# A two-layer hybrid encoder on one core: filler per step, the place of two modulation sums, and the queue place of the value loads

## The chip, the cores and the metric

The kernel runs on one core of a Trainium2 chip. The metric is the device time in microseconds (us). The core's engines have queues of their own and each works its queue strictly in order: PE (matrix products and the transposes made with them), DVE (vector), ACT (scalar functions), POOL (elementwise work and the "low halves" of split operands) and SP, whose queue issues all DMAs of this kernel. They wait for each other by semaphores only.

## The reference

Sequence 1024, width 1024, two layers, everything in float32:

```python
for l in range(2):
    shift, scale, gate = split(silu(c) @ ada_w[l] + ada_b[l], 3)
    h = rms_norm(x, norm_g[l]) * (1 + scale) + shift
    if l == 0:   # differential attention (4 heads, two softmax maps each)
                 # beside a bidirectional RG-LRU; both gated; one output projection
        y = even_mixer(h, ...)
    else:        # 2-D neighbourhood attention, 16 heads, 8 x 16 window; gated
        y = odd_mixer(h, ...)
    x = x + gate * y
return rms_norm(x, final_g)
```

## The kernel before

Every large product is done as three products of split operands: an operand is kept as a high half (rounded for PE) and a low half (the remainder), and hi·hi, hi·lo and lo·hi are added up in one PSUM bank. One **projection product** here means one weight slab (128 output rows, 1024 inputs) times one half of the tokens (512): 8 blocks of the input width times 3, so 24 matrix instructions of 128x512. A slab passes three stations before PE can use it: a DMA of 512 KB into `raw` (two buffers), ACT's copy to `whi` (L185), POOL's subtraction to `wlo` (L186).

The kernel runs in stages: a start, the RG-LRU with most of layer 0's projections, layer 0's attention, the "boundary" (layer 0's output projection, the residual sum and layer 1's norm), neighbourhood attention, and the last output projection with the final norm.

**Attention (layer 0).** It is cut into 32 units, one for each head and block of 128 queries. A unit has two sets of logits (tiles `s`, L659 and L660), bias and minimum on DVE (L927), the exponential on ACT (L931), a combination of both maps on DVE and POOL (L946, L948, L949), transposes (`atr`, L957) with their split on ACT and DVE (L964, L965), and for every second unit the product with the values (`o`). Four times in each unit `step()` calls `feed.pump(PUMP)`: a credit of `PUMP` nanoseconds is added, and projection work of a queue called `feed` is put into the program until the credit is spent. The feed holds 19 half-slab products of four pieces with 1300 credit each: 98,800 in all. The loop makes 33 x 4 = 132 steps. At the end of each unit one turn of a modulation generator follows.

**Boundary.** `out_layer(0, ...)` gives `r0` and `r1`: eight projection products for each half of the tokens, over the slabs of `wo0`. The written program is put in order by a scheduler that takes ready instructions by priority, so the first product of `r0` (called pp24 below, the next pp25 and so on up to pp39, by slab) already stands between the last units of attention. Its inputs are the four attention outputs and four RG-LRU outputs `y`, which come back from DRAM (L1128) once attention's key buffers are free, and are split on ACT and POOL (L225, L226). Beside the products, `mod_part` makes two pieces of layer 1's modulation (the scale): each of eight turns loads 256 KB of `ada` (L322) and DVE adds it, weighted, to `macc` (L334, L336); then come `wait` empty turns; then PE sums `macc` over the partitions (tile `mrow`, L368), ACT copies the row (L348), PE turns it into a column (L353) and DVE adds the bias (L356, L358). `wait` is an entry of `NW`. After each product of `r0` three turns are taken. `tail(0, ...)` uses the scale: it makes layer 1's input for the first half of the tokens, one block after another between the products of `r1`.

**Neighbourhood attention (layer 1).** The value projection of two head pairs is one job, `v1_job`: eight blocks of tokens (t = 0 to 7), each evicted to a tile `vt` of two buffers and written to DRAM (`vd`, L1196). `load_v` reads the values back in another order, four blocks for each pair (tiles `vc`, L1208), and `na_c` multiplies with them (tile `no`, L1330). All writes, loads, slabs and biases go through SP's one queue, and an instruction there that waits for a landing holds everything behind it. A load needs the writes of the token blocks that it reads: the first needs t = 5, the second t = 6, the third t = 7.

What sets the order around the change: the numbers `PUMP` and `NW`, the calls of `some(mod, n)` in the boundary, and priorities of the scheduler (`tc.issue_after(x)` gives what follows a place right behind instruction x).

Of the kernel before, what the change touches and what calls it, by code (L numbers as in the profile page):

```python
# [19 lines left out]
P = 128  # L20
# [6 lines left out]
LR = 13  # L27
SQ = 8
NM = (2, 2, 2)
NW = (3, 3, 3, 3)  # L30
KORDER1 = (6, 0, 1, 2, 3, 4, 5, 7)
PUMP = 800.0
PUMP1 = 4400.0
LATE = 3

# [62 lines left out]
def kernel(ctx, tc, xT, xTp, small, lamp, adaw, tb, w0, gw, wo0, w1, nab, wo1, out):  # L98
    nc = tc.nc
# [14 lines left out]
    vd = dram.tile([S, D], F32, tag="vd", name="vd")  # L114
# [17 lines left out]
    def make_sel(pool):  # L132

        sel = state["sel"] = pool.tile([P, 4, P], F32, tag="sel", name="sel", bufs=1)
        G.memset(sel[:], 1.0)
        G.affine_select(sel[:], sel[:], pattern=[[-32, 4], [0, P]], base=0,
                        channel_multiplier=1, compare_op=ALU.is_equal, fill=0.0)
# [11 lines left out]
    state = {"load": 0, "split": 0, "third": None, "turn": 2, "wide": True, "bank": 0}  # L149
# [41 lines left out]
    def slab(i):  # L191
        while state["split"] <= i:
            split_next()
        return ready[i]

    def ahead(i):
        if state["split"] <= i:
            split_next()
# [38 lines left out]
    def proj(i, hf, evac, korder=range(KC), prep=True, view=lambda x: x, cols=(0, HF)):  # L237
        ks = list(korder)
        wh, wl = slab(i)
        ps = bank(f"pp{i}_{hf}")[:, :cols[1] - cols[0]]  # L240
        for n, k in enumerate(ks):
            hi, lo = (t[:, cols[0]:cols[1]] for t in hact[k, hf])
            mm3(ps, wh[:, k, :], wl[:, k, :], view(hi), view(lo), n == 0, n == KC - 1)
            if n % 2 == 1 and n < KC - 1:
                yield 1300.0
        with tc.high_priority():
            evac(hf, ps)
        if prep:
            ahead(i + 1)
        yield 1300.0  # L250
# [362 lines left out]
    def evac_k(key):  # L613
        def f(hf, ps):
            if hf == 0 or (key, 0) not in ks_:
                ks_[key, 0] = kqp.tile([P, S], F32R, tag="ks0", name="ks0")
                ks_[key, 1] = kqp.tile([P, S], F32R, tag="ks1", name="ks1")
            def dst(t, b):
                x = t[b:b + 64, hf * HF:(hf + 1) * HF]
                return x if key[0] == "a" else by_tile(x)  # L620

            def src(b):
                x = ps[b:b + 64, :]
                return x if key[0] == "a" else x.rearrange("p (b g y) -> p b g y", g=2, b=4)

            k0, k1 = ks_[key, 0], ks_[key, 1]
            A.activation(dst(k0, 0), src(0), AF.Copy)
            A.activation(dst(k1, 64), src(64), AF.Copy)
            V.tensor_tensor(dst(k0, 64), src(0), dst(k0, 0), ALU.subtract)
            V.tensor_tensor(dst(k1, 0), src(64), dst(k1, 64), ALU.subtract)  # L630
        return f

    def evac_q(key):

        def f(hf, ps):
            q0 = kqp.tile([P, HF], F32R, tag="qq0", name="qq0", bufs=3)
            q1 = kqp.tile([P, HF], F32R, tag="qq1", name="qq1", bufs=3)

            l0 = kqp.tile([P, HF], F32R, tag="qlo", name="ql0", bufs=3)
            l1 = kqp.tile([P, HF], F32R, tag="qlo1", name="ql1", bufs=3)  # L640
            G.memset(l0[64:128, :].bitcast(F32), 0.0)
            G.memset(l1[0:64, :].bitcast(F32), 0.0)
            A.activation(q0[0:64, :], ps[0:64, :], AF.Copy, scale=0.125)
            A.activation(q1[64:128, :], ps[64:128, :], AF.Copy, scale=0.125)
            V.scalar_tensor_tensor(l0[0:64, :], ps[0:64, :], 0.125, q0[0:64, :],
                                   ALU.mult, ALU.subtract)
            V.scalar_tensor_tensor(l1[64:128, :], ps[64:128, :], 0.125, q1[64:128, :],
                                   ALU.mult, ALU.subtract)
            nc.sync.dma_start(q0[64:128, :].bitcast(F32), q0[0:64, :].bitcast(F32))
            nc.sync.dma_start(q1[0:64, :].bitcast(F32), q1[64:128, :].bitcast(F32))  # L650
            qs_[key, hf] = (q0, q1, l0, l1)
        return f
# [17 lines left out]
    def mods(n, pool, **kw):  # L670

        for _ in range(n):
            yield from mod_part(*later_mods.popleft(), pool, **kw)

    def some(gen, n):
        for _ in range(n):
            next(gen, None)

    def after_dve(gen, n):

        with tc.issue_after(state["dve"]):
            some(gen, n)
# [176 lines left out]
    with ExitStack() as l0:  # L859
# [144 lines left out]
        def step():  # L1004
            if later and next(later[0], 0) == 0:
                later.popleft()
            feed.pump(PUMP)

        mod = mods(NM[1], ap, bufs=1, wait=NW[1])
        for u in range(33):  # L1010
# [97 lines left out]
    def evac_g1(p, pool, tag="sq", late=False):  # L1108
        def f(hf, ps):
            c = slice(hf * HF, (hf + 1) * HF)  # L1110
            t = pool.tile([P, HF], F32, tag=tag, name="sg1", bufs=3)
            if late:
                silu2(hf, ps, t, t)
                state["gated1"][p, hf] = t
                state["gate1"](p, hf)
            else:
                if hf == 0:
                    mix_tile(p, f"sg1_{p}")
                silu2(hf, ps, t, mixed[p][:, c])
        return f  # L1120
# [10 lines left out]
    with tc.tile_pool(name="bound", bufs=2) as bp:  # L1131
        make_sel(bp)
        run, tail = out_layer(0, ato0, xTp, x1d, bp, [4, 5, 6, 7, 0, 1, 2, 3], by_fours, by_tile,
                              ((0, 0, 0, HF), (KC, 1, 0, HF)))
        r0, r1 = run(0), run(1)
        mod = mods(NM[2], bp, bufs=4, wait=NW[2])
        for c in range(KC):
            some(r0, 1)
            after_dve(mod, 3)
        some(mod, 99)  # L1140

        t0 = tail(0, to_h1)
        for c in range(KC):
            some(r1, 1)
            some(t0, (1, 1, 2, 2, 2, 2, 0, 0)[c])
        t1 = tail(1, to_h1)
        ev = {"k": evac_k(("b", 0)), "q": evac_q(("b", 0)), "g": evac_g1(0, bp)}
        first = lambda key, hf: proj(at1[key, 0], hf, ev[key], prep=False)
        ahead(at1["q", 0])
        some(first("k", 0), 99)  # L1150
        some(t1, 1)
        ahead(at1["g", 0])
        some(first("q", 0), 99)
        some(t1, 1)
        for _ in first("g", 0):
            some(t1, 2)
        k1, q1 = first("k", 1), first("q", 1)
        for _ in range(5):
            some(k1, 1)
            some(q1, 1)  # L1160
        ahead(at1["g", 0] + 1)
        some(first("g", 1), 99)
        ahead(at1["g", 0] + 2)
# [3 lines left out]
    with ExitStack() as l1:  # L1167
# [7 lines left out]
        vd4 = vd[:].rearrange("(g y) e -> g y e", g=4)  # L1175

        def v1_job(p):

            i = at1["v", p]
            ws = [slab(i), slab(i + 1)]  # L1180
            for t in range(8):
                hf, b = divmod(t, 4)
                ps = bank("v1")
                for k in range(KC):
                    hi, lo = (t[:, b * P:(b + 1) * P] for t in hact[k, hf])
                    wh, wl = (w[:].rearrange("p (k a) n -> p k (a n)", a=2)[:, k % 4, :]
                              for w in ws[k // 4])
                    mm3(ps[:, :256], hi, lo, wh, wl, k == 0, k == KC - 1)
                    if k == 3:
                        yield 1300.0  # L1190
                vt = ap.tile([P, 256], F32, tag="vt", name="vt", bufs=2)
                if t % 2:
                    A.activation(vt[:], ps[:, :256], AF.Copy)
                else:
                    V.tensor_copy(vt[:], ps[:, :256])
                nc.sync.dma_start(vd4[2 * hf:2 * hf + 2, 64 * b:64 * b + 64, P * p:P * p + 256],  # L1196
                                  vt[:])
                if t == 1:
                    ahead(i + 2)
                yield 1300.0  # L1200

        def load_v(p, b):
            if (p, b) in vch or p == NA_PAIRS:
                return
            w = BLK_W[b]
            vt = vch[p, b] = vp.tile([P, 4, P], F32, tag="vch", name=f"vc{p}_{b}")
            y = slice(4 * BLK_C0[b], 4 * (BLK_C0[b] + w))
            nc.sync.dma_start(vt[:4 * w], vd4[:, y, P * p:P * p + P].rearrange("g y e -> y g e"))  # L1208

        def load_ahead(p):  # L1210

# [133 lines left out]
        n_units = 8 * NA_PAIRS  # L1345
        mod = mods(2, ap, tag="tmp", bufs=3, acc=(ap, "tmp"), wait=NW[3], early=True)
        es, ets = {0: na_a(0)}, {}
        for u in range(n_units + 1):
# [4 lines left out]
            if u % 8 == 2:  # L1353

                p = u // 8
# [138 lines left out]
```

## Time and profile before

| | us |
|---|---|
| three runs | 1206.6, 1210.18, 1210.3 |
| median | 1210.18 |
| the profiled execution | 1210.03 |
| its span, first to last instruction | 1208.0 |
| PE busy in the span | 1151.2 (95%) |
| DVE busy | 728.8 (60%) |
| ACT busy | 566.6 (47%) |
| POOL busy | 387.0 (32%) |

PE is busy almost all the time. What a change can win is the time in which PE stands idle, and the time after it in which the granted clock of PE is lower. The profile's "idle before" and "waits" name the last event that let an engine go on; "issue" there means that the profile shows no event.

### The profile page before, as it was taken

Reading aid. Unit: us, or ns where it says so; the run is one execution under the profiler, and the core shown is the slowest. Engines: PE = TensorE matmul, PEld = TensorE weight load, DVE = VectorE, ACT = ScalarE, POOL = GpSimd, SP = SyncE. Lnnn points to the kernel's source line nnn. Section 1 sums busy time; section 2 is a strip of 40 time slices with the busy share of each in tenths; the row PEclk is TensorE's granted clock in tenths of the full one; section 3 lists DMA queues with packets and bytes.
Section 4 is the critical chain, followed back from the end, with each engine's and each line's share of the span. In section 5 each row is a group of like instructions: output and inputs, shape, how many; then the busy total and the mean of one; then the engine's idle time right before and its main releaser. Section 6 shows DMA issues by size and latency. Waiting matters only on the chain.

```text
span 1208.0 us, 19169 instructions
## 1 busy us (share of the span) xinstructions
PE 1151.2 (95%) x7232; PEld 980.0 (81%) x7232; DVE 728.8 (60%) x1414; ACT 566.6 (47%) x1031; POOL 387.0 (32%) x354
## 2 busy tenths in 40 slices
PE   4999999999999999779999899999999999999996
PEld 3788778888778887657879788988998898888896
DVE  6757949588889889658873244333444434546354
ACT  4357586466555558423433344334444434445121
POOL 2124421332323344524423332332333333216200
PEclk8999999999999999889999999999999999999998
DMA  9723132322121110276523432343445444214212
GB/s 329 228 73 122 51 94 77 94 82 75 38 86 53 58 46 21 67 231 222 179 74 117 130 93 86 94 141 101 128 132 141 136 128 132 78 52 150 99 71 71
DMA packets 82045, 132.26 MB, mean 109 GB/s; under 512 B 7584, under 2 KB 48672, under 8 KB 81952
## 3 DMA queue, kind: packets, MB, share of 16 engines
q1 hardware_dynamic: 81952, 131.03, 34.8%
q8 instruction: 57, 0.93, 0.3%
q14 instruction: 36, 0.29, 0.1%
HBM read 110.03 MB, written 14.68 MB: 103 GB/s over the span
## 4 chain that ended last, share of the span: by engine, by line
PE 78%; DVE 9%; DMA 4%; issue 4%; ACT 3%; POOL 2%; SPq 0%; DVEq 0%; POOLq 0%; ACTq 0%
PE pp L201 16%; PE pp L202 16%; PE pp L203 15%; PE no L1330 3%; PE etr L1312 3%; PE v L201 2%; PE v L202 2%; PE v L203 2%; PE atr L957 2%; DMA vd<-vt 2%; PE s L659 2%; PE s L660 2%; PE n L659 2%; PE n L660 2%; DVE e L927 1%
## 5 line engine op out<-in xcount | busy, mean ns | idle before, releaser
L202 PE MATMUL pp<-alo,whi 128*128 128x512 f32 (+1 forms) x1040 | 395.0, 380 | 3.6 <-POOL alo L226 3.6
L201 PE MATMUL pp<-ahi,whi 128*128 128x512 f32 (+1 forms) x1040 | 397.2, 382 | 0.2 <-DVE ks L630 0.2
L203 PE MATMUL pp<-ahi,wlo 128*128 128x512 f32 (+1 forms) x1040 | 394.8, 380 | 1.0 <-POOL wlo L186 1.0
L186 POOL TENSOR_TENSOR wlo<-raw,whi 128x1024 fp32r<-128x1024 f32 x80 | 197.5, 2472 | 268.5 <-ACT whi L185 254.5
L202 PEld LDWEIGHTS pp<-alo,whi 128*128 128x128 f32 x1040 | 197.1, 189 | 37.6 <-POOL alo L226 4.3
L203 PEld LDWEIGHTS pp<-ahi,wlo 128*128 128x128 f32 x1040 | 196.7, 189 | 38.1 <-POOL wlo L186 1.8
L201 PEld LDWEIGHTS pp<-ahi,whi 128*128 128x128 f32 x1040 | 196.9, 189 | 35.7 <-issue 2.1
L1301 POOL TENSOR_SCALAR e<-e,r 128x288 f32<-128x288 f32 (+1 forms) x128 | 71.3, 570 | 239.7 <-DVE r L1299 239.3
L185 ACT ACTIVATE whi<-raw 128x1024 fp32r<-128x1024 f32 x80 | 84.3, 1056 | 121.0 <-PE pp L202 65.7
L1296 ACT ACTIVATE e<-e,nm 128x288 f32<-128x288 f32 (+1 forms) x128 | 72.7, 569 | 51.3 <-DVE nm L1293 50.7
L931 ACT ACTIVATE e<-e,nm 128x1024 f32<-128x1024 f32 x64 | 73.5, 1149 | 47.7 <-DVE nm L927 45.5
L1293 DVE CUSTOM_DVE_ANT_0 e<-n,bias 128x288 f32<-128x288 f32 (+1 forms) x128 | 60.4, 504 | 51.9 <-PE n L660 32.2
L1318 DVE COPY e<-etr 96x384 f32<-96x384 f32 (+1 forms) x64 | 35.5, 554 | 91.1 <-PE etr L1312 89.5
L1316 ACT ACTIVATE e<-etr 96x384 f32<-96x384 f32 (+1 forms) x64 | 31.3, 490 | 118.9 <-DVE e L1318 118.5
L927 DVE CUSTOM_DVE_ANT_0 e<-s,tb 128x1024 f32<-128x1024 f32 x64 | 77.1, 1219 | 10.1 <-PE s L660 9.1
L201 PE MATMUL v<-whi,ahi 128*128 128x256 f32 x256 | 72.2, 282 | 0.0
L203 PE MATMUL v<-whi,alo 128*128 128x256 f32 x256 | 71.9, 281 | 0.0
L202 PE MATMUL v<-wlo,ahi 128*128 128x256 f32 x256 | 71.9, 281 | 0.0
L948 POOL TENSOR_SCALAR e<-e,r 128x256 f32<-128x256 f32 x32 | 33.9, 1059 | 110.1 <-DVE r L937 47.2
L964 ACT ACTIVATE ath<-atr 128x512 fp32r<-128x512 f32 x64 | 37.7, 596 | 40.4 <-PE atr L957 40.0
L1062 DVE SCALAR_TENSOR_TENSOR xh<-pp,mod,xh 128x512 f32<-128x512 f32 (+1 forms) x40 | 25.7, 641 | 50.8 <-PE pp L203 49.9
L1067 ACT ACTIVATE sq<-xh 128x512 f32<-128x512 f32 (+1 forms) x40 | 21.7, 543 | 72.8 <-DVE xh L1062 71.9
(207 smaller groups left out, 2076.4 us busy)
## 6 DMA issues: line engine op xcount, KB each, us to landing
raw<-in_w_dram SPq DMA_DIRECT2D x56, 512.0 KB
ada<-in_adaw_dram SPq DMA_DIRECT2D x96, 256.0 KB
raw<-in_wo_dram SPq DMA_DIRECT2D x24, 512.0 KB
bias<-in_nab_dram SPq DMA_DIRECT2D x64, 144.0 KB
qq<-qq SPq DMA_DIRECT2D x48, 128.0 KB
bias<-in_nab_dram SPq DMA_DIRECT2D x32, 192.0 KB
xT<-in_xT_dram SPq DMA_DIRECT2D x16, 256.0 KB
xh<-in_xTp_dram SPq DMA_DIRECT2D x16, 256.0 KB
```

Of the source, the lines that this page charges most:

```text
L185: A.activation(hi[:], raw[:], AF.Copy)
L186: G.tensor_tensor(lo[:], raw[:], hi[:], ALU.subtract)
L201: T.matmul(ps, lh, rh, start=start, stop=False)
L202: T.matmul(ps, lh, rl, start=False, stop=False)
L203: state["pe"] = T.matmul(ps, ll, rh, start=False, stop=stop).ins
L659: T.matmul(dst, qsel(q[m]), k, start=True, stop=False)
L660: T.matmul(dst, qsel(q[2 + m]), k, start=False, stop=True)
L927: state["dve"] = V.tensor_tensor_reduce(out=e[:], in0=ps[:].rearrange("p a b -> p (a b)"), in1=tbt[h][:, o:o + S], scale=-1.0, scalar=3.0e ...
L931: A.activation(e[:], e[:], AF.Exp, scale=-1.0, bias=nm[:], accum_out=sums[:, m:m + 1])
L1293: state["dve"] = V.tensor_tensor_reduce(out=e[:, m, :n], in0=ps[:, m, :n], in1=bias["now"][m][:, :n], scale=-1.0, scalar=3.0e38, op0=ALU.a ...
L1296: A.activation(e[:, m, :n], e[:, m, :n], AF.Exp, scale=-1.0, bias=nm[:, m:m + 1], accum_out=sums[:, m:m + 1])
L1301: state["pool"] = G.tensor_scalar(e[:, m, :n], e[:, m, :n], r[:, m:m + 1], 0.0, ALU.mult, ALU.add).ins
```

## The change

Three independent edits.

1. `PUMP` falls from 800 to 745. Over 132 steps that is a credit of 98,340 instead of 105,600, against 98,800 of work: the attention filler is dealt out more thinly and reaches the loop's end instead of ending in the 31st unit.
2. The third entry of `NW` rises from 3 to 7, so each of the boundary's two modulation pieces takes 16 turns instead of 12. The first piece's sum on PE now follows the sixth product of `r0`, not the fourth. The second piece no longer ends before `r1`: its last waits and its sum are taken behind the first and second product of `r1`.
3. `load_v` stands in `tc.issue_after(state["vd"])`, where `state["vd"]` is the last write of a value block so far.

```diff
-NW = (3, 3, 3, 3)
+NW = (3, 3, 7, 3)
-PUMP = 800.0
+PUMP = 745.0
...
             after_dve(mod, 3)
-        some(mod, 99)
...
             some(r1, 1)
+            some(mod, (4, 99)[c] if c < 2 else 0)
             some(t0, (1, 1, 2, 2, 2, 2, 0, 0)[c])
...
-                nc.sync.dma_start(vd4[2 * hf:2 * hf + 2, 64 * b:64 * b + 64, P * p:P * p + 256],
-                                  vt[:])
+                state["vd"] = nc.sync.dma_start(
+                    vd4[2 * hf:2 * hf + 2, 64 * b:64 * b + 64, P * p:P * p + 256], vt[:]).ins
...
-            nc.sync.dma_start(vt[:4 * w], vd4[:, y, P * p:P * p + P].rearrange("g y e -> y g e"))
+            with tc.issue_after(state["vd"]):
+
+                nc.sync.dma_start(vt[:4 * w],
+                                  vd4[:, y, P * p:P * p + P].rearrange("g y e -> y g e"))
```

On PE, behind the last logits of attention (`s_1_4660`, the second map of the last unit), there stood so far the first output product pp24 (`pp_0_4880`), whose third input block is already the reloaded `y` tile `ahi_0_4820`; `obc` and `atr` belong to attention:

```order
L660 MATMUL s_1_4660<-ks_3055,ql_3474 128x512
L201 MATMUL pp_0_4880<-ahi_0_4812,whi_4471 128x512
L202 MATMUL pp_0_4880<-alo_0_4813,whi_4471 128x512
L203 MATMUL pp_0_4880<-ahi_0_4812,wlo_4472 128x512
L201 MATMUL pp_0_4880<-ahi_0_4816,whi_4471 128x512
L397 MATMUL obc<-osq,sel 128x128 x4
L957 MATMUL atr<-ident,e_0_4490 128x128 x4
L202 MATMUL pp_0_4880<-alo_0_4817,whi_4471 128x512
L203 MATMUL pp_0_4880<-ahi_0_4816,wlo_4472 128x512
L201 MATMUL pp_0_4880<-ahi_0_4820,whi_4471 128x512
```

Now there stands the feed's last half-slab product (`pp_1_4648`, the last gate), whose inputs were made long before:

```order
L660 MATMUL s_1_4632<-ks_3126,ql_3597 128x512
L201 MATMUL pp_1_4648<-ahi_1_489,whi_4328 128x512
L202 MATMUL pp_1_4648<-alo_1_490,whi_4328 128x512
L203 MATMUL pp_1_4648<-ahi_1_489,wlo_4329 128x512
L201 MATMUL pp_1_4648<-ahi_1_494,whi_4328 128x512
L202 MATMUL pp_1_4648<-alo_1_495,whi_4328 128x512
L203 MATMUL pp_1_4648<-ahi_1_494,wlo_4329 128x512
L201 MATMUL pp_1_4648<-ahi_1_634,whi_4328 128x512
L397 MATMUL obc<-osq,sel 128x128 x4
L957 MATMUL atr<-ident,e_0_4446 128x128 x4
```

All 24 instructions of that product now come behind the last logits, and pp24 behind them. So 24 product instructions fewer stand ahead of the last logits. Behind attention's last `obc` there were 3 instructions of pp25 left so far, and there are 21 now.

On SP, in the boundary, the slab of pp29 (`raw_5052`) stood behind the write of the residual block 3 (`x1d<-xh_0_3`):

```order
L1065 DMA x1d<-xh_0_2_4925 128x512
L322 DMA ada<-in_adaw_dram 128x512 x2
L1053 DMA xh_0_4_5016<-in_xTp_dram 128x512
L1065 DMA x1d<-xh_0_3_4972 128x512
L156 DMA raw_5052<-in_wo_dram 128x1024
L1053 DMA xh_0_5_5062<-in_xTp_dram 128x512
L156 DMA raw_5098<-in_wo_dram 128x1024
L322 DMA ada<-in_adaw_dram 128x512 x3
```

Now the slabs of pp29 and pp30 (`raw_5052`, `raw_5090`) are ahead of that write:

```order
L1065 DMA x1d<-xh_0_2_4925 128x512
L322 DMA ada<-in_adaw_dram 128x512 x2
L1053 DMA xh_0_4_5016<-in_xTp_dram 128x512
L156 DMA raw_5052<-in_wo_dram 128x1024
L1053 DMA xh_0_5_5054<-in_xTp_dram 128x512
L156 DMA raw_5090<-in_wo_dram 128x1024
L1065 DMA x1d<-xh_0_3_4972 128x512
```

The write of block 3 and three loads of the second modulation piece moved behind the slabs.

On SP, in the first value job of layer 1, the loads `vc` stood between the last writes (the row `x3` ends with t = 5):

```order
L1196 DMA vd<-vt 2x64x256 x3
L1208 DMA vc_0_6210<-vd 96x4x128
L1196 DMA vd<-vt 2x64x256
L1208 DMA vc_1_6212<-vd 128x4x128
L156 DMA raw_6454<-in_w_dram 128x1024
L1196 DMA vd<-vt 2x64x256
L1269 DMA bias<-in_nab_dram 128x288
L1269 DMA bias<-in_nab_dram 128x384
L156 DMA raw_6584<-in_w_dram 128x1024
L1208 DMA vc_2_6214<-vd 128x4x128
```

Now all writes come first, up to t = 7, with one slab between the last two:

```order
L1196 DMA vd<-vt 2x64x256 x4
L156 DMA raw_6454<-in_w_dram 128x1024
L1196 DMA vd<-vt 2x64x256
L1210 DMA vc_0_6210<-vd 96x4x128
L1210 DMA vc_1_6212<-vd 128x4x128
L1272 DMA bias<-in_nab_dram 128x288
L1210 DMA vc_2_6214<-vd 128x4x128
L1210 DMA vc_3_6216<-vd 96x4x128
L1272 DMA bias<-in_nab_dram 128x384
```

The two loads went behind the writes of t = 6 and t = 7, and the third and fourth went ahead of one bias load and one slab. The other three value jobs change in the same way; in the last of them only one load moves. On PE, DVE, ACT and POOL nothing is moved in layer 1.

## The prediction

> **What bounds the kernel now.** The page comes first: busy times of the engines, then the span in 40 slices of 30.2 us.
>
> ```profile
> span 1208.0 us, 19169 instructions
> PE 1151.2 (95%) x7232; PEld 980.0 (81%) x7232; DVE 728.8 (60%) x1414; ACT 566.6 (47%) x1031; POOL 387.0 (32%) x354
> PE   4999999999999999779999899999999999999996
> PEclk8999999999999999889999999999999999999998
> ```
>
> PE is the bound nearly everywhere. The two 7s in its row, with two 8s in the clock row below, are 483 to 543 us: the end of attention and the start of the boundary. The edits touch nothing else that waits, except the value loads from 640 on. So the second view is windows of 5 us at these places. The columns are the busy us of PE, PEld, DVE, ACT and POOL, then the granted clock, the DMA share and GB/s.
>
> ```profile
> 470.00:475.00 5.00, 4.56 (x36) 2.97 (x34) 4.96 (x9) 4.19 (x8) 1.18 (x2) 1.00 0.00 0
> 475.00:480.00 5.00, 3.31 (x10) 2.83 (x11) 4.45 (x11) 1.77 (x3) 2.06 (x3) 0.67 0.00 0
> 485.00:490.00 5.00, 2.40 (x18) 2.08 (x18) 4.79 (x11) 4.74 (x5) 3.58 (x5) 1.00 0.56 193
> 490.00:495.00 5.00, 1.39 (x7) 0.67 (x5) 5.00 (x8) 2.95 (x5) 5.00 (x5) 0.88 0.00 2
> 495.00:500.00 5.00, 4.96 (x22) 4.87 (x23) 3.04 (x5) 1.18 (x3) 4.19 (x3) 0.50 0.02 3
> 525.00:530.00 5.00, 2.51 (x12) 1.74 (x10) 4.94 (x6) 0.63 (x1) 2.45 (x1) 1.00 0.92 291
> 530.00:535.00 5.00, 0.15 (x4) 0.18 (x8) 4.14 (x7) 0.63 (x1) 0.00 (x0) 0.63 0.94 280
> 535.00:540.00 5.00, 5.00 (x20) 3.67 (x16) 0.16 (x1) 1.33 (x2) 0.46 (x1) 0.50 0.90 302
> 540.00:545.00 5.00, 5.00 (x21) 4.04 (x20) 0.72 (x2) 0.90 (x1) 1.91 (x1) 0.84 0.72 257
> 680.00:685.00 5.00, 4.33 (x40) 3.47 (x38) 0.47 (x2) 0.51 (x2) 0.00 (x0) 1.00 0.56 192
> 685.00:690.00 5.00, 2.27 (x24) 1.81 (x24) 2.03 (x4) 2.62 (x6) 3.33 (x3) 0.83 0.76 205
> 690.00:695.00 5.00, 5.00 (x21) 4.33 (x20) 1.90 (x6) 1.31 (x4) 0.88 (x2) 0.83 0.30 98
> 795.00:800.00 5.00, 4.17 (x54) 3.35 (x54) 1.12 (x4) 1.11 (x3) 0.99 (x2) 1.00 0.76 202
> ```
>
> PE's idle time in a window is 5.00 less its first number; what a low clock costs is that busy number times (1 - clock). **Tail of attention**: idle 0.44 + 1.69 + 2.60 + 3.61 = 8.3, clock 3.31 x 0.33 + 1.39 x 0.12 + 4.96 x 0.50 = 3.7, together 12.0 us. **Boundary**: idle 2.49 + 4.85 = 7.3, clock 5 x 0.50 + 5 x 0.16 = 3.3, together 10.6. **Value loads**: idle 0.67 + 2.73, clock 2.27 x 0.17 + 5 x 0.17 = 1.2, and 0.83 at 795, together 5.5. The sum, 28.1 us, is the ceiling of the whole change: PE's own work stays what it is.
>
> Third, the waits of PE: who released it, total us, times, longest.
>
> ```profile
> PE mrow L368 <- issue: 7.3, 1, 7.3
> PE pp L202 <- POOL alo L226: 3.6, 2, 3.2
> PE obc L397 <- DVE osq L384: 2.6, 1, 2.6
> PE atr L957 <- DVE atl L965: 1.9, 1, 1.9
> PE no L1330 <- DMA vc<-vd: 4.2, 3, 3.4
> ```
>
> Each edit has its wait: the modulation sum (mrow) 7.3, the value loads (vc) 4.2. The tail is mixed: 3.6 us for the reloaded y blocks split on POOL, but 4.5 us for DVE.
>
> **Edit 1, the filler.** No instruction is added. 24 product instructions leave the front of the last logits, so units come to their end earlier if DVE can follow.
>
> ```profile
> 400.00:450.00 50.00, 50.00 (x316) 41.72 (x315) 43.21 (x97) 27.59 (x52) 17.09 (x19) 1.00 0.20 63
> ```
>
> Here PE is full and DVE has 6.8 us of 50 left, so the units before the tail do speed up. In the tail it is the other way round: DVE is busy 4.96, 4.45, 4.79 and 5.00 of 5, so more PE work there does not make DVE's chain shorter. What the last gate product behind the last logits covers for certain is the wait for y: 24 instructions are more than the 3.6 us. With it would go the half clock that follows it at 495:500, 2.5 us. That is one end, 6.1. The other end is 0: the last combine, which waits for DVE, makes PE wait as long at the same place. I take 3.5, a little above the middle, because the y wait is certain to be covered and only the DVE wait behind it is open. For the range the ends are 0 and all 12.0.
>
> **Edit 2, the sums.** Here are the sum's own rows on DVE and PE, and SP, ACT and POOL on the slab of pp29, with the evictions of pp28 and pp29 as last rows.
>
> ```profile
> 514.76 1.16 PE L397 MATMUL obc<-osq,sel 128*128 128x128 f32 x8
> 530.04 0.42 SPq L1053 DMA_DIRECT2D xh<-in_xTp_dram  x1
> 532.62 0.38 SPq L156 DMA_DIRECT2D raw<-in_wo_dram  x1
> 534.00 0.74 DVE L336 SCALAR_TENSOR_TENSOR macc<-ada,ctmp,macc 128x512 f32<-128x512 f32 x1
> 534.85 0.65 PE L368 MATMUL mrow<-macc,ones 128*32 128x128 f32 x8 [7.34 <-issue]
> 538.41 1.06 ACT L185 ACTIVATE whi<-raw 128x1024 fp32r<-128x1024 f32 x1 [2.57 <-DMA raw<-in_wo_dram]
> 539.54 2.37 POOL L186 TENSOR_TENSOR wlo<-raw,whi 128x1024 fp32r<-128x1024 f32 x1 [12.09 <-ACT whi L185]
> 544.28 0.75 DVE L1062 SCALAR_TENSOR_TENSOR xh<-pp,mod,xh 128x512 f32<-128x512 f32 x1 [7.61 <-PE pp L203]
> 549.72 0.75 DVE L1062 SCALAR_TENSOR_TENSOR xh<-pp,mod,xh 128x512 f32<-128x512 f32 x1 [0.23 <-PE pp L203]
> ```
>
> "issue" hides the releaser, but mrow starts 0.1 us after DVE's eighth accumulation has ended (534.74): the sum asks for macc too early. A product takes 549.72 - 544.28 = 5.44 us, so two products later the sum asks 10.9 us later, at 538.4 by the old clock, and macc is there. **What is late next** is the slab of pp29: ACT waits for its DMA until 538.41, and the DMA engines are at 0.92 and 0.94. So far this lies under the 7.34 us. Counted from the obc at 514.76, which is shortly before the boundary's loads may start: the slab is issued at +17.9, split by ACT from +23.7 and by POOL until +27.2 (541.91). In the new order it follows xh directly, so it is issued at 530.46 or +15.7, 2.2 us sooner, with whi done at +22.6 and wlo at +25.0. PE has 1.16 of obc, then 21 + 72 instructions at 5.44 / 24 = 0.227 until pp29: +22.2. It waits 0.4 for whi, makes two products, and waits for wlo until +25.0: 2.4 us idle, though with 18 instructions (4.1 us) of its work moved behind the obc. The new place has a price too. The row of the sum is copied by ACT behind the split of the slab of pp31, itself a DMA; PE's L353 waits behind 4 instructions of pp30, and DVE's L356 behind that. I estimate 1.0 us, the length of one split (1.06). The second sum, L353 behind the first bc, costs under 0.5, and the scale it gives is needed only by layer 1's first product, six products later. So the boundary's 10.6 becomes 2.4 + 1.0 and a half microsecond of clock: gain 6.7, with ends 2 (the slab comes no sooner) and 10.6.
>
> The 535:540 row shows the clock at 0.50 behind 7.34 us of idle, and the 475:480 row 0.67 in and around 1.69. The Trainium skill ("TensorE: Matmul & The Clock Gate", "What's actually happening") says that PE falls to half clock after an idle window of about 3.4 us and needs as long a busy one to recover. The first row agrees, the second does not need that much idle. By the page the 2.4 us cost no clock and the gain is 7.2; by the second row 1.1, and it is 6.1.
>
> **Edit 3, the loads.** SP's queue of the first value job, POOL, and the end of the chain of work:
>
> ```profile
> 669.28 2.42 POOL L186 TENSOR_TENSOR wlo<-raw,whi 128x1024 fp32r<-128x1024 f32 x1 [9.68 <-issue]
> 670.15 0.34 SPq L1208 DMA_DIRECT2D vc<-vd  x1
> 670.53 0.49 SPq L1196 DMA_DIRECT2D vd<-vt  x1
> 675.62 0.39 SPq L1208 DMA_DIRECT2D vc<-vd  x1
> 676.11 0.86 SPq L156 DMA_DIRECT2D raw<-in_w_dram  x1
> 677.06 0.50 SPq L1196 DMA_DIRECT2D vd<-vt  x1
> 677.06 6.54 DMA vd<-vt
> 683.61 4.08 DMA vc<-vd
> ```
>
> The second load sits in the queue until 675.62, where the write of t = 6 has landed, and the slab and the write of t = 7 behind it. Then come 6.54 us of landing and 4.08 of load, until 687.69. Without the loads ahead of it the slab waits only for POOL's split, which ends at 671.70; the write of t = 7 follows at about 672.3, 4.8 us sooner, and the third load lands at 672.3 + 6.54 + 4.08 = 682.9. PE went idle at 684.3 (685 - 0.67), so the wait goes with 1.4 us to spare. The biases and the slab behind the loads are issued 1 to 2 us later than now; what hides them is PE's work, and if that is not enough they cost as much. Of 5.5 I take 4.7; the ends are 0 and 5.5.
>
> **Sum.** 3.5 + 6.7 + 4.7 = 14.9. From the profiled execution's 1210.03 that is 1195.1, so I say **1195**; the median of the runs shown, 1210.18, is the same to 0.2, while one of them was 1206.6.
>
> **Rivals.**
> *The tail goes entirely.* Against it stand DVE's full windows; for it, that the units come earlier and y is loaded earlier. 12.0 + 6.7 + 4.7 = 23.4: 1187.
> *New waits take the place of the old ones.* DVE holds the tail (0), the slabs hold the boundary (2), only the loads are won (4.7): 1203. For it: DVE busy at 5.00 and the DMA share of 0.94 in the very windows that are to be won.
> *The change doesn't do what it says.* The loads land together and late, the sums wait at L353: under 3 us, 1208.
> *Slower.* DVE becomes the bound of all of attention: with less filler each unit waits for DVE once, as at 475:480, where one such wait cost 1.69 + 1.1 = 2.8 us. It decides where the 28 units before the tail lose 14.9 / 28 = 0.53 us each on average; at 0.7 it is 19.6 lost, 1215. Against it: the 6.8 us that DVE has free in 50.
>
> **How the numbers follow.** Forecast 0.52, tail gone 0.20, new waits 0.17, nothing 0.07, slower 0.04. About 0.3%, 3.6 us, can be told from no change, so all below 1206.5 counts as faster: 0.89, same 0.07, slower 0.04. The range runs from 1185, two below the tail's case, to 1206, three above the case of new waits; what is left out is nothing, slower, and the edges.
>
> **What would show it.** In the changed profile: no wait of mrow near 7 us, a PE wait of 2 to 3 us on wlo or whi in pp29; the pp L202 wait on alo gone and PE still idle before the last atr of attention; the wait of no on vc under 1 us, with t = 7 written within 5 us of t = 6. I am wrong if PE's idle time grows before the tail, if the boundary's slabs make it wait more than once, or if the last combine costs nothing.

## The result, and the profile after

The changed kernel took 1196.8 us (median of 7 runs, 1194.3 to 1203.9) beside 1209.3 of the kernel before: ratio 0.9911, 95% interval 0.9888 to 0.9935. A second set of runs gave 1197.9 beside 1207.1: 0.9923 (0.9900 to 0.9947). So by these ratios the change wins 9.3 to 10.7 us of about 1208 (the medians of the two sets lie 12.5 and 9.2 apart); a gain of 14.9 had been forecast. The profiled execution took 1195.79; its start happened to come 2.0 us sooner than that of before, as the ledger below shows.

The page of after: span, busy times, then PE and its clock in 40 slices of 29.9 us.

```profile
span 1194.1 us, 19182 instructions
PE 1145.0 (96%) x7232; PEld 975.6 (82%) x7232; DVE 728.8 (61%) x1414; ACT 566.9 (47%) x1031; POOL 387.7 (32%) x354
PE   4999999999999999799999999999999999999996
PEclk8999999999999999899999999999999999999998
```

Of the two 7s one is left, the end of attention; the boundary's is gone. PE has as many instructions as before. Its busy time is 6.2 us shorter, and the granted clock accounts for 5.6 of that: busy time x (1 - clock), summed over windows of 5 us, is 13.6 us before and 8.0 after.

The windows that answer to those of before (busy us of PE, PEld, DVE, ACT, POOL, then clock, DMA share, GB/s):

```profile
350.00:400.00 50.00, 45.10 (x259) 37.74 (x258) 42.04 (x82) 26.38 (x48) 13.73 (x15) 0.97 0.23 70
475.00:480.00 5.00, 3.50 (x16) 2.57 (x14) 5.00 (x9) 5.00 (x7) 4.64 (x4) 1.00 0.57 172
480.00:485.00 5.00, 1.39 (x6) 1.39 (x7) 5.00 (x6) 0.76 (x1) 3.32 (x4) 0.61 0.09 38
485.00:490.00 5.00, 5.00 (x27) 4.42 (x26) 3.83 (x6) 3.17 (x5) 0.32 (x1) 0.71 0.00 0
490.00:495.00 5.00, 4.04 (x29) 3.38 (x27) 4.51 (x6) 5.00 (x10) 2.80 (x2) 1.00 0.01 2
495.00:500.00 5.00, 3.97 (x23) 3.22 (x24) 4.83 (x9) 4.81 (x8) 3.61 (x4) 1.00 0.01 3
530.00:535.00 5.00, 2.31 (x10) 1.30 (x9) 2.25 (x4) 3.15 (x4) 2.59 (x2) 1.00 0.75 288
535.00:540.00 5.00, 5.00 (x16) 3.94 (x16) 2.64 (x1) 0.00 (x0) 2.09 (x1) 0.66 0.81 252
685.00:690.00 5.00, 5.00 (x28) 4.17 (x26) 1.74 (x5) 2.19 (x6) 1.15 (x2) 1.00 0.45 111
```

The value loads' stretch (685) is full. The boundary has one short stall. The tail still stands idle with DVE at 5.00 of 5. And the first row is new: 4.9 us idle in the middle of attention, 3.1 at a product `s` and 1.8 at the next obc. The same window of before:

```profile
350.00:400.00 50.00, 49.22 (x291) 41.38 (x290) 44.22 (x86) 27.99 (x49) 15.05 (x14) 1.00 0.20 63
```

The waits of PE in after (total us, times, longest) name the largest of these. Of the 7.2 at obc, 5.1 stand in the tail and 1.8 in the middle of attention; of the 2.8 on wlo, 1.7 stand in the boundary's stall, and the other 1.1, near 607 us, had been 1.0 before:

```profile
PE obc L397 <- DVE osq L384: 7.2, 3, 5.1
...
PE s L659 <- DVE nm L927: 3.1, 1, 3.1
PE pp L203 <- POOL wlo L186: 2.8, 2, 1.7
...
PE pp L201 <- ACT whi L185: 1.0, 1, 1.0
```

For a ledger I cut every profile at three marks: the first logits product of attention (L659), the last obc of attention (**T0**) and the first value product of layer 1. Loss is summed over windows of 5 us between the marks: 5 less PE's busy time, plus busy time x (1 - clock). The last 50 us before T0 are the tail. "Start" is the time up to the first mark, which no edit touches. All in us:

| profile | start | attention's body | tail | boundary | rest |
|---|---|---|---|---|---|
| before | 227.3 | 3.3 | 12.5 | 12.5 | 16.3 |
| after | 225.3 | 7.3 | 9.3 | 5.8 | 11.1 |
| after less before | -2.0 | **+4.0** | -3.2 | -6.7 | -5.2 |

PE's own work at full clock is 936.1 us before and 935.3 after, so the columns make up 13.1 of the 13.9 us between the spans. Of the tail's 3.2, idle time is the smaller part: it fell from 8.4 to 7.3, the loss by the clock from 4.1 to 2.1. The start is chance: over the 14 profiles of this study it lies between 224.9 and 228.5, whatever the kernel.

### The profile page after: what moved, and what is told of

Its sections match the earlier page's. It is cut to its first block, busy times and chain, and to the rows that moved or that the text cites. A ratio compares the mean times of both kernels' runs of the same rounds, so it can differ in the third digit from the quotient of the medians.

```text
span 1194.1 us, 19182 instructions
## 1 busy us (share of the span) xinstructions
PE 1145.0 (96%) x7232; PEld 975.6 (82%) x7232; DVE 728.8 (61%) x1414; ACT 566.9 (47%) x1031; POOL 387.7 (32%) x354
## 4 chain that ended last, share of the span: by engine, by line
PE 77%; DVE 12%; ACT 4%; DMA 3%; issue 2%; POOL 1%; SPq 0%; DVEq 0%; ACTq 0%; POOLq 0%
PE pp L201 15%; PE pp L202 15%; PE pp L203 15%; PE no L1333 4%; PE etr L1315 3%; PE v L201 3%; PE v L203 2%; PE v L202 2%; DVE e L927 2%; PE n L659 2%; PE atr L957 2%; PE n L660 2%; PE s L659 1%; PE s L660 1%; POOL wlo L186 1%
## 5 line engine op out<-in xcount | busy, mean ns | idle before, releaser
L927 DVE CUSTOM_DVE_ANT_0 e<-s,tb 128x1024 f32<-128x1024 f32 x64 | 77.5, 1219 | 11.3 <-DMA tb<-in_tb_dram 4.6
L659 PE MATMUL s<-ks,qq 128*128 128x512 f32 x128 | 52.8, 413 | 3.1 <-DVE nm L927 3.1
```

The source lines that it names most:

```text
L659: T.matmul(dst, qsel(q[m]), k, start=True, stop=False)
L927: state["dve"] = V.tensor_tensor_reduce(out=e[:], in0=ps[:].rearrange("p a b -> p (a b)"), in1=tbt[h][:, o:o + S], scale=-1.0, scalar=3.0e ...
```

## Experiments

Each was timed beside the kernel before (its median 1207.1 to 1208.4 in the three sets), and its loss was taken at the same marks:

| run | ratio to before, 95% | body | tail | boundary | rest |
|---|---|---|---|---|---|
| e1, filler alone | 0.9992 (0.9977 to 1.0007) | 7.6 | 9.4 | 9.0 | 15.9 |
| e2, sums alone | 1.0012 (0.9995 to 1.0029) | 3.3 | 12.5 | 13.0 | 16.5 |
| e3, after without loads | 0.9975 (0.9957 to 0.9993) | 8.2 | 9.5 | 5.8 | 15.6 |
| e4, tb in pieces | 0.9903 (0.9887 to 0.9919) | 6.1 | 9.4 | 7.5 | 10.0 |
| e5, splits on DVE | 0.9952 (0.9922 to 0.9981) | 8.8 | 7.7 | 12.3 | 10.0 |
| e6, thin ada | 0.9887 (0.9858 to 0.9916) | 7.6 | 9.4 | 2.4 | 10.5 |
| e7, fewer Newton steps | 0.9904 (0.9871 to 0.9938) | 7.7 | 5.1 | 4.4 | 10.2 |
| e8, obc later | 0.9898 (0.9860 to 0.9936) | 8.0 | 8.7 | 4.4 | 10.0 |
| after, again | 0.9923 (0.9900 to 0.9947) | 8.0 | 9.4 | 6.0 | 10.5 |
| e9, tb and ada | 0.9878 (0.9852 to 0.9904) | 4.1 | 9.4 | 2.4 | 10.2 |
| e10, tb, ada and obc | 0.9873 (0.9843 to 0.9903) | 4.1 | 9.6 | 2.5 | 9.9 |
| e11, old filler, thin ada | 0.9930 (0.9908 to 0.9953) | 3.3 | 12.5 | 11.3 | 9.4 |

The ratio is of several runs, the loss of one profile each. Before lost 44.6 in all four columns. For e3, e7 and e9 the gain by the ledger lies above the upper end of the ratio's interval, by 0.3, 1.6 and 0.6 us; the profiled executions of e7 and e9 were the fastest of their sets. So the ledger says where time went, and the ratio what a kernel is worth.

### The edits one by one

**e1**, the filler alone:

```diff
-PUMP = 800.0
+PUMP = 745.0
```

> The kernel before with the thinner filler alone (745 for 800). Theory A: the start of the boundary, the obc behind attention, comes 5.6 us sooner (509.12 for 514.76 in the trace of after), and the boundary runs by its DMAs from there on, so that the 18 product instructions (4.1 us) that were moved behind the obc lie inside the wait of mrow, which shrinks from 7.3 to about 3.2. Time about 5.6 under the kernel before: ratio 0.995. Theory B, the prediction's terms taken apart as they stand: the edit wins 2.7 in the tail and loses about 5 in attention's body to the wait for tb (0 to 3.5 by the prediction), mrow waits 7 as before. Ratio 0.997 to 1.002.

**e2**, the sums alone:

```diff
-NW = (3, 3, 3, 3)
+NW = (3, 3, 7, 3)
...
-        some(mod, 99)
...
+            some(mod, (4, 99)[c] if c < 2 else 0)
```

> The kernel before with the sums two products later alone. Theory A: PE comes to pp29 18 instructions sooner, at +18 us from the obc, while its slab is split at +25 as in after: PE waits 6 to 7 us for whi and wlo in place of mrow's 7.3, and the clock falls behind it. Gain 1 to 3: ratio 0.9975 to 0.999. Theory B, the prediction's term: the wait is 2 to 3 us, gain 6.2 to 6.7, ratio 0.9945 to 0.995.

In e1, T0 came 284.0 us behind the first mark, 3.4 sooner than before (287.4), mrow waited 4.3 in place of 7.3, and the boundary lost 3.5 less although no edit was made there. In e2 the wait of mrow is gone and this stands in its place: PE's rows at pp29, and two windows of e2.

```profile
539.09 0.80 PE L201 MATMUL pp<-ahi,whi 128*128 128x512 f32 x1 [6.19 <-ACT whi L185]
541.52 0.79 PE L203 MATMUL pp<-ahi,wlo 128*128 128x512 f32 x1 [1.21 <-POOL wlo L186]
```

```profile
535.00:540.00 5.00, 0.91 (x2) 0.50 (x2) 1.19 (x2) 1.69 (x2) 0.88 (x1) 0.73 0.87 297
540.00:545.00 5.00, 3.79 (x9) 2.80 (x9) 0.00 (x0) 1.06 (x1) 3.79 (x2) 0.50 0.55 184
```

On the waits theory A comes out in both: mrow shrinks in e1 (to 4.3, where 3.2 was expected), and in e2 there are 7.4 us of waiting for the slab of pp29 in place of 7.3 for mrow. On the time it misses in both: e1's 0.9992 is in theory B's range, since attention's body lost 4.3 more, and e2's 1.0012 is above both. Neither edit alone can be told from nothing in time (e1 wins 1.0 by its ratio, between -0.8 and 2.8), while the two together (e3) win 3.0 (0.8 to 5.2). In e2 PE stands at the slab from +19.0 us behind T0 and has whi at +25.2; in after it comes at +22.3 and has whi at +23.3. So the slab is split at a time that does not follow PE's pace (it is issued at +18.8 in e2 and at +16.2 in after); the 18 products (4.1 us) that the thinner filler leaves behind T0 are what covers most of it once the sums no longer stand in the way. In the ledger the boundary gains 3.5 by the filler, loses 0.5 by the sums, and gains 6.7 by both.

**e3**, after with the loads as before:

```diff
-            with tc.issue_after(state["vd"]):
-                nc.sync.dma_start(vt[:4 * w], ...)
+            nc.sync.dma_start(vt[:4 * w], ...)
```

> The kernel after, with the value loads issued without their place behind the last value write, as before. If the loads are worth what the two traces differ in from 640 us on, the waits of no on vc come back with 4 us and the time rises by 5.3 (prediction's term 4.7): 1202, ratio to before 0.994 to 0.995. Rival: the other two edits shift the value jobs so that the waits don't come back; ratio 0.991 as after.

The waits on vc came back with 3.1 us, and the rest of the kernel, from the first value product on, took 563.6 us, as in before (563.7), e1 (563.4) and e2 (564.1). In the profiles that have the edit it took 555.7 to 557.7. So the edit is worth 6 us or more by the length of this stage, and 6.3 to 7.7 by the ratios (0.9975 less 0.9911 or 0.9923), more than the 5.3 expected; the ledger finds 4.5 to 5.1 of it as idle time and clock.

### What the filler cost in attention

The load of the third head's bias table (tb, 960 KB) on SP and the first bias and minimum of that head on DVE, before:

```profile
354.61 0.33 SPq L855 DMA_DIRECT2D tb<-in_tb_dram  x1
361.83 1.21 DVE L927 CUSTOM_DVE_ANT_0 e<-s,tb 128x1024 f32<-128x1024 f32 x1
```

The same two in after, and the product on PE that waits for DVE:

```profile
349.49 0.33 SPq L855 DMA_DIRECT2D tb<-in_tb_dram  x1
357.11 1.22 DVE L927 CUSTOM_DVE_ANT_0 e<-s,tb 128x1024 f32<-128x1024 f32 x1 [3.67 <-DMA tb<-in_tb_dram]
358.40 0.80 PE L659 MATMUL s<-ks,qq 128*128 128x512 f32 x1 [3.13 <-DVE nm L927]
```

The table has one buffer, so its load is issued when the last unit of the head ahead has read the old one. Before, the new head needed it 7.2 us behind the issue; in after, with less filler between, it would have 4.0 us behind it (357.11 - 3.67 - 349.49), and got it after 7.6. **e4** loads it in pieces, as the units of the old head leave its columns:

```diff
...
+            if m and h < DA_HEADS - 1:
+                if qt == 6:
+                    tb_cols(h + 1, 1024, 1920)
+                if qt == 7:
+                    tb_cols(h + 1, 896, 1024)
+                    tb_cols(h + 1, 0, 896)
```

> The kernel after, with the bias table of a head (tb) loaded in three pieces, the first one unit sooner and the one that the head's first unit needs besides it, 64 KB, next. Theory A: the wait of DVE for tb (4.6 us, the new idle time of PE at 350 to 400) is what the thinner filler cost in attention's body; without it the obc behind attention comes 4 to 6 us sooner and the time falls by as much: 1191 to 1193, ratio 0.985 to 0.987. Rival: DVE was about to be late there anyway (24.0 of 25 us busy at 375 to 400); PE waits as long for DVE a few units on, and the gain is under 1.5: ratio 0.990 or 0.991.

DVE's wait fell from 3.67 to this, in e4:

```profile
354.22 1.23 DVE L931 CUSTOM_DVE_ANT_0 e<-s,tb 128x1024 f32<-128x1024 f32 x1 [0.93 <-DMA tb<-in_tb_dram]
```

PE's wait fell to 0.4, and T0 stood 282.2 us behind the first mark in place of 283.8. That is less than half of theory A, and the boundary gave back 1.7. The time, 0.9903, is what the rival had said, but its mechanism does not account for it: at the next obc PE waited 2.0 us for DVE, and 1.8 in after too. In e9, with the same attention, DVE had no wait for tb left, the body lost 4.1 and T0 came at 279.8 (280.3 in e10): there theory A's 4 us are whole. The middle of attention in e9, whole and where the next obc stands:

```profile
350.00:400.00 50.00, 47.47 (x294) 39.97 (x296) 46.47 (x91) 29.47 (x55) 14.83 (x16) 1.00 0.23 64
375.00:380.00 5.00, 3.00 (x20) 2.42 (x19) 4.83 (x9) 1.57 (x3) 3.86 (x3) 1.00 0.64 143
```

The 2.0 us at the obc are there too, but the clock stays at 1.00, where e4 had 0.85 and 0.81 in the two windows from 375 to 385. Of the 2.0 us between the two bodies 1.4 are clock and 0.6 idle time; why the clock fell in one and not in the other is open.

That the thin filler and the load in one piece cost 3 to 4 us in attention is shown by the profiles: the body loses 7.3 to 8.8 in the eight with both, 3.3 in the three with the old filler (before, e2, e11), and 4.1, 4.1 and 6.1 in the three with the load in pieces. The timed runs don't show this size: e4 is 1.0 to 2.4 us under after by the ratios and e9 1.1 under e6, with intervals wider than that.

### What holds the tail

**e7** leaves two of three Newton steps out of the inverse root behind the tail's obc, **e8** moves that obc behind other work, **e5** takes POOL's splits of y to DVE:

```diff
-            rr = rstd_rows(ss, 128, ap, sq, 0.0)
+            rr = rstd_rows(ss, 128, ap, sq, 0.0, 1 if h == 3 and hf == 0 else 3)   # e7
...
+            rr_ins = [state["pe"]]                                                 # e8
...
+            if h == 3 and hf == 0:
+                yield
+                yield
+                yield
-            spread(rr, bc)
+            with tc.issue_after(state["pe"] if h == 3 and hf == 0 else rr_ins[0]):
+                spread(rr, bc)
...
-                          G if l == 0 and k >= 4 else V, order)
+                          V, order)                                                # e5
```

> The kernel after, with two of three Newton steps left out in the inverse root that the obc in the tail waits for (six 128x128 operations of DVE; the half of one head is scaled with less precision). They took 4.3 us there, 3.2 of it two rows of 1.60 beside POOL. The order on PE changes with it: the obc is placed one logit product sooner. Theory A: DVE's queue holds the tail; with 4.3 us less in it the tail loses 3 to 4 us less and the last obc comes as much sooner: ratio 0.988 to 0.989. Theory B: the y blocks (their load, POOL's splits) or the combine are late next; the wait moves on to atr or pp, less than 1.5 us is won: 0.990 or 0.991.

> The kernel after, with that obc of the tail placed later on PE, behind both transposes of unit 30, which now stand ahead of the last logits; no work is added or left out. Theory A (DVE's queue holds the tail): PE waits for DVE at the transposes instead, and the idle time of the tail stays within 1.5 us of after's 7.3; time within 1.5 us of after, ratio 0.990 to 0.992. Theory B (the obc stands too early on PE, and there is other work that it keeps back): the wait of 5.1 goes, idle time in the tail falls by 3 or more, ratio 0.988 or less.

> The kernel after, with the low parts of the reloaded y blocks (8 subtractions, 128x512) on DVE instead of POOL. PE's order has the same products, 13 of them ahead of the last obc instead of behind it. Theory A: in the tail DVE is held up beside POOL's subtractions (L383 takes 1.60 beside them and 0.28 alone, L226 2.44 and 0.7 to 1.1), 7 us in all at 470 to 500, more than the 8 x 0.69 = 5.5 us that DVE would take over; the stretched rows are gone, the wait of obc falls from 5.1 to 3 or less, and the tail loses 3 to 5 us less. Since the slab of pp29 comes at +25 from the last obc whatever PE does, the time follows the last obc: 1 to 3 us under after, ratio 0.989 to 0.990. Theory B: DVE's own work is the bound, 5.5 us more of it on DVE makes the wait of obc longer (7 or more) and the time 2 to 5 us longer: ratio 0.993 to 0.995.

DVE's rows in after's tail, with POOL's two splits of y at the same time:

```profile
475.21 2.44 DVE L226 TENSOR_TENSOR alo<-vT,ahi 128x512 fp32r<-128x512 f32 x1
477.58 1.60 DVE L383 TENSOR_TENSOR osq<-osq 128x128 f32<-128x128 f32 x1
480.35 0.28 DVE L383 TENSOR_TENSOR osq<-osq 128x128 f32<-128x128 f32 x1
481.96 1.60 DVE L384 SCALAR_TENSOR_TENSOR osq<-osq 128x128 f32<-128x128 f32 x1
```

```profile
475.07 3.96 POOL L226 TENSOR_TENSOR alo<-y,ahi 128x512 fp32r<-128x512 f32 x2 [4.60 <-ACT ahi L225]
481.65 1.76 POOL L226 TENSOR_TENSOR alo<-y,ahi 128x512 fp32r<-128x512 f32 x1
```

The same operation takes 0.28 alone and 1.60 beside POOL. The Trainium skill ("SBUF — State Buffer", "SBUF: two separate sides") says that a DVE operation with two SBUF inputs and a POOL operation that reads SBUF exclude each other for a whole instruction. The rows agree, and so does e5, where POOL splits no y there:

```profile
479.48 1.09 DVE L226 TENSOR_TENSOR alo<-y,ahi 128x512 fp32r<-128x512 f32 x1
480.49 0.28 DVE L383 TENSOR_TENSOR osq<-osq 128x128 f32<-128x128 f32 x1
...
482.55 0.28 DVE L384 SCALAR_TENSOR_TENSOR osq<-osq 128x128 f32<-128x128 f32 x1
```

The stretched rows are gone, and the wait of 5.1 at the obc with them:

```profile
485.63 1.16 PE L397 MATMUL obc<-osq,sel 128*128 128x128 f32 x8 [1.50 <-DVE osq L384]
```

But DVE has eight more operations in the tail, and PE waits for it elsewhere: 1.4 at the transposes behind this obc, 1.3 at later ones, and 2.1 at the last obc, where another row of DVE's chain is stretched beside a slab split of POOL (509.89 to 512.29; the row took 0.23 in after):

```profile
510.12 2.25 DVE L379 TENSOR_SCALAR osq<-osq 128x128 int32<-128x128 int32 x1
```

The idle time of the tail is 7.7 us, for 7.3 in after. That its loss is 7.7 for 9.3 is the clock, which stayed at 1.00 in e5 and cost 2.1 in after. And 13 products stand ahead of T0 again, so that at pp29 of e5 PE waits longer:

```profile
541.23 0.79 PE L201 MATMUL pp<-ahi,whi 128*128 128x512 f32 x1 [6.46 <-ACT whi L185]
543.67 0.80 PE L203 MATMUL pp<-ahi,wlo 128*128 128x512 f32 x1 [1.22 <-POOL wlo L186]
```

The boundary loses 12.3. Theory A was right on the stretched rows and on the wait at the obc, and wrong on the idle time of the tail and on the time, which came out as theory B had it from another cause. The expectation took the slab's time from T0 as fixed, and it is not: from T0 = 515.4 the slab is issued at +18.4 (+16.2 in after) behind three ada loads that held SP's queue for 5.0 us, and PE has whi at +25.8. To the missing cover of 3.0 us come about 2.0 for the later slab and 1.5 for the low clock.

In e7 the obc goes with almost no wait:

```profile
476.64 1.13 PE L397 MATMUL obc<-osq,sel 128*128 128x128 f32 x8 [0.25 <-DVE osq L384]
```

The tail's idle time falls from 7.3 to 5.2, no clock is lost behind it, and T0 comes 280.4 behind the first mark, 3.4 sooner than in after: theory A by the profile. The time doesn't tell the theories apart: 0.9904 is theory B's figure, and its interval, 0.9871 to 0.9938, of four runs, holds both. In e8 the wait is only divided: 3.1 at the obc and 2.7 at the products behind it, 6.1 us of idle time in all. PE's rows of e10, which has the same order there:

```profile
477.71 1.87 PE L397 MATMUL obc<-osq,sel 128*128 128x128 f32 x8 [3.13 <-DVE osq L384]
...
495.28 0.58 PE L201 MATMUL o<-ath,vh 128*128 128x256 f32 x1 [2.83 <-DVE atl L975]
```

So by the profiles DVE's queue holds the tail, and how PE's work is placed around it changes little (T0 0.4 sooner in e8, 0.5 later in e10 than in e9).

### What holds the boundary

**e6** thins the ada loads that stand ahead of the slab of pp29:

```diff
-            after_dve(mod, 3)
+            after_dve(mod, (1, 1, 2, 2, 2, 8, 4, 4)[c])
```

> The kernel after, with the modulation's weights (ada, 256 KB each) loaded more thinly in the boundary: 1, 1, 2, 2 and 2 behind the first five products instead of 3, 3, 2 behind the first three; the sums stay where they are. Theory A: the slab of pp29 is late because the ada loads share the DMA engines with it and stand before it in SP's queue; four loads fewer ahead of it (1 MB, 3 us at 290 to 330 GB/s) bring it 2 to 3 us sooner, the waits for whi and wlo (1.0 + 1.7) and the low clock behind them (1.7) go, and the boundary is 3 to 4.5 us shorter: T0 to the first value product 123 to 124 instead of 127.3, ratio 0.987 to 0.989. Theory B: the slab waits for its buffer, free only when POOL has split the slab ahead (523.9), and then takes its time to land; the wait stays above 2 us, the time within 1 us of after.

After and e6 at this slab: in after, from T0 = 509.12, PE reaches pp29 at +22.3 and gets its two halves at +23.3 and +25.7.

```profile
509.12 1.16 PE L397 MATMUL obc<-osq,sel 128*128 128x128 f32 x8
532.38 0.50 PE L201 MATMUL pp<-ahi,whi 128*128 128x512 f32 x1 [0.98 <-ACT whi L185]
534.82 0.50 PE L203 MATMUL pp<-ahi,wlo 128*128 128x512 f32 x1 [1.70 <-POOL wlo L186]
541.64 0.43 PE L368 MATMUL mrow<-macc,ones 128*32 128x128 f32 x8
543.03 0.28 PE L353 MATMUL mrow<-pick,macc 128*128 128x4 f32 x2
```

In e6, from T0 = 511.0, ACT and POOL split the slab by +20.3 and +22.7:

```profile
530.22 1.06 ACT L185 ACTIVATE whi<-raw 128x1024 fp32r<-128x1024 f32 x1 [5.31 <-DMA raw<-in_wo_dram]
531.36 2.39 POOL L186 TENSOR_TENSOR wlo<-raw,whi 128x1024 fp32r<-128x1024 f32 x1 [5.51 <-ACT whi L185]
```

PE waits for neither. From T0 to the first value product it is 123.6 us in place of 127.3, and the ratio is 0.9887, both as theory A had it. **e9** puts e4 and e6 together, **e10** e8 as well; **e11** is e6 with the old filler.

> The kernel after with both remedies that won something alone: the bias table in pieces and the thin ada loads. Theory A (the boundary runs by the slab that comes a set time behind the last obc, so that a win in attention is kept whole, and the slab's own win comes on top): stage of attention 282.2, boundary 123.6 to 124.5, 5 to 6 us under after: ratio 0.986 to 0.987. Rival: with the obc sooner the slab is late again, and one of the two wins is lost: 0.988 or more.

> The same, and the obc of the tail later on PE. That alone moved the wait from obc to the products behind it and changed the length of attention by 0.4 us. Theory A (DVE's queue holds the tail): no more than 1 us from the kernel without it. Theory B (some of what PE can do is kept back): 2 us or more.

> The kernel after with the old filler (800) and the thin ada loads: what the thinner filler is worth where the slab of pp29 comes sooner. Theory A (the filler's worth is the 18 products that it leaves behind the obc as cover for the slab): attention is 287.3 long, PE comes to pp29 4.1 us sooner, at +18, and waits there about 4 us for whi (+20.3) and wlo (+22.7), with a low clock behind it: boundary 124 to 126, time 3 to 5 us above the thin ada loads with the new filler, ratio 0.991 to 0.993. Theory B (the filler wins in attention itself): the boundary is 4.1 us shorter, 119.5, as its work is, and the time is within 1 us of that kernel: 0.988 or 0.989.

> The kernel after, unchanged, on the chip and beside the runs of before that the next three kernels share. Its runs spread from 1194 to 1204 the first time. If the change is worth the first result, the ratio is 0.991 again; the start of the kernel (to the first logits product of attention), which the change leaves alone, came 2.0 us sooner in the profile of after than in that of before: if that was chance, the ratio may well be 0.992 to 0.993.

In its profile e9 keeps both wins (attention 279.8, boundary 123.5). It takes 1192.9 beside 1197.9 of after in the same set, and its ratio, 0.9878, lies between theory A's and the rival's; e6 alone had 0.9887. e10 takes 1190.2, which its interval does not part from e9. Both are faster than before, and by their medians 5 to 8 us faster than after. e11 is 5 us slower than e6, as theory A said, but only half in its way. PE's rows of e11:

```profile
531.38 0.50 PE L201 MATMUL pp<-ahi,whi 128*128 128x512 f32 x1 [0.82 <-ACT whi L185]
533.92 0.50 PE L203 MATMUL pp<-ahi,wlo 128*128 128x512 f32 x1 [1.80 <-POOL wlo L186]
...
567.00 2.08 PE L397 MATMUL bc<-rr,sel 128*128 128x128 f32 x8 [3.32 <-DVE rr L384]
```

The slab costs 2.6 where 4 were expected, since whi was there at +19.0 behind T0 and not at +20.3, and the first bc of layer 1's norm waits 3.3 for DVE, which neither theory had. Within attention the new filler is no gain at all by the ledger: 7.6 + 9.4 lost in e6, 3.3 + 12.5 in e11.

## Why the prediction was right, and where it was not

The time fell inside the range, near the forecast, and most of what was to show it is there: no wait of mrow, none on alo, none on vc, PE idle for 1.0 us before the last transposes of attention. By the ledger the three terms come out in size and one loss was not in the sum: 3.5 + 6.7 + 4.7 = 14.9 stand against 3.2 + 6.7 + 5.2 = 15.1, less 4.0 in attention's body, so 11.1; the timed gain is 9.3 to 10.7. The profiled execution hid this, since its start came 2.0 us sooner by chance. That the sizes agree so closely is partly luck, as the first and third point say.

- **Ceiling of the tail and "24 instructions are more than the 3.6 us".** The wait on alo is gone, as predicted, and DVE makes PE wait at the obc instead (5.1). The tail won 3.2, near the middle that was taken, but only 1.1 of it is idle time; the rest is clock, and how much clock a stall costs varied here. The bound is DVE's queue, by the profiles of e7 and e8. That DVE's rows are stretched beside POOL is shown too, but in e5, without POOL's splits, the waits moved and did not become less.
- **"Here PE is full and DVE has 6.8 us of 50 left, so the units before the tail do speed up."** This is the step that failed. It looked at one window and one engine. At the third head the units came so much sooner that the load of tb was late. By the ledger the sum should have carried about -4 here. The sign that the prediction named (PE's idle time grows before the tail) is what the profile showed. The rival "slower" had the right place, the body of attention, with the wrong mechanism: a loss at one head's change, not at each of 28 units.
- **The boundary.** The chain was right to 0.7 us: whi foreseen at +22.6 and there at +23.2, wlo at +25.0 and +25.7, PE at +22.2 and +22.3, 2.4 us idle foreseen and 2.68 measured (3.43 in the second profile of after). The price of 1.0 for the sum's second matrix product (L353) did not appear; about 1 us more of low clock stood against it, so it is luck that the 6.7 came out whole. What was wrong is whose gain it is. The 6.7 were booked on the sums, and the 4.1 us of products "moved behind the obc" were noted and not priced. e2 shows that the sums alone win nothing: PE then stands at the slab 3.3 us earlier, and the slab comes 1.9 later.
- **The clock behind it.** The half microsecond of the sum was 1.3 to 1.7. The Trainium skill's idle window of 3.4 us ("TensorE: Matmul & The Clock Gate", "What's actually happening") would have it at nothing; by the 475:480 row of before it was 1.1. Here the row was nearer. But e7 and e8 idled 3.0 and 2.9 us at the same place with the clock at 1.00 behind it, so neither tells a single case.
- **The loads.** The mechanism was right: the slab is issued before the last write, which no load holds up any more, and the write of t = 7 follows that of t = 6 by 4.0 us in place of 6.5. The size was 5.2 by the ledger and 6 to 7 by e3, for 4.7. The ceiling of 5.5 counted the two largest stalls only: with them (4.8 and 0.8 by the ledger) went a third, of 0.5 near 915 us, and a new wait of 0.9 came, of `no` for ACT near 1087.

SP's rows of after for the last point: the slab, the two writes around it and the loads behind the second.

```profile
660.25 0.48 SPq L1196 DMA_DIRECT2D vd<-vt  x1
...
663.84 0.34 SPq L156 DMA_DIRECT2D raw<-in_w_dram  x1
664.27 0.49 SPq L1196 DMA_DIRECT2D vd<-vt  x1
664.86 1.00 SPq L1210 DMA_DIRECT2D vc<-vd  x2
```

## What to carry to other kernels

When work is moved from ahead of a late point to behind it, price it in both stages: behind T0 it was cover for a slab, and without it (e2) the edit that seemed to win the boundary won nothing. When filler is thinned out, follow every load that is issued at one event and needed at a later one (here 7.2 us apart, with one buffer): the distance shrinks with the filler, and the engine's own free time says nothing of it. And compare stages between marks, not spans: 2 us of this difference arose where no edit was.

## What the runs showed of the hardware

The start of the kernel, where the DMA share is 0.93 in the first 50 us, took 224.9 to 228.5 us to the same instruction in 14 profiles, so a single profile is good to about 2 us here. DVE's 128x128 operation with two SBUF inputs took 0.28 alone and 1.60 beside POOL's 128x512 subtraction, and without POOL's eight subtractions it took 0.28 or 0.29 throughout (e5). DVE's L379, 0.23 in after, took 2.25 in e5 beside POOL's 128x1024 subtraction. Idle stretches of 2.7 to 3.0 us at one place were followed by a clock of 0.66 over 5 us in after, of 0.80 and 0.86 in two windows of 5 us in e3, and of 1.00 in e7 and e8.
